# First linear of both MLPs: input parts side by side under the high weights, blocks of 256 outputs

## The chip, the cores and the metric

One NeuronCore of a Trainium2 chip runs the whole program. The metric is the device time of one execution in microseconds. Of the kernel before there are three timed runs, and one more execution was recorded by the hardware profiler.

## What is computed

Two layers of an encoder trunk on 256 tokens of width 2048 in float32. Each layer is a mixer (layer 0: a long convolution beside gated linear attention; layer 1: RWKV-7) followed by an MLP of width 8192. The change is in the MLPs:

```python
def adaln(x, c, norm_g, ada_w, ada_b):
    m = jax.nn.silu(c) @ ada_w + ada_b
    shift, scale, gate = jnp.split(m[:, None, :], 3, axis=-1)
    return rmsnorm(x, norm_g) * (1.0 + scale) + shift, gate

def sqrelu_mlp(h, w1, w2):
    return jnp.square(jax.nn.relu(h @ w1)) @ w2
...
        h, gate = adaln(x, c, ffn_norm_g[layer], ffn_ada_w[layer], ffn_ada_b[layer])
        x = x + gate * sqrelu_mlp(h, ffn_w1[layer], ffn_w2[layer])
```

Here h is 256 x 2048, w1 is 2048 x 8192 and w2 is 8192 x 2048. "First linear" is h @ w1, "second linear" is the product with w2.

## The kernel before

**Products in three parts.** The large matmuls run on operands of type float32r. So that little is lost, each float32 operand is split into a high part (a cast to float32r on ScalarE, line 465) and a low part (the float32 value minus the high part, line 466, on VectorE for weights and on GpSimd for activations). A product is then three matmuls that add up in PSUM: high x high, high x low and low x high. The function `prod` writes them (lines 504, 505, 506). Every matmul loads its own 128x128 of stationary operand first.

**Normalised input.** `norm_steps` (line 419 and on) makes h transposed, features on the partitions: 16 tiles of 128 features x 256 tokens. Eight steps make two tiles each: transposing matmuls (line 439), the high part by ScalarE (line 453), the full value by VectorE (line 457), and the low part by GpSimd (line 458). Before the change the high parts of tiles 0 to 7 lie in one buffer, their low parts in another, and tiles 8 to 15 in two more.

**First linear.** `ffn` goes through the 8192 hidden features in two halves. In each half `feat_block` makes eight blocks of 512 outputs. A block holds two PSUM buffers (tiles named f_mm), each with two groups of 128 outputs x 256 tokens; the pool has four such buffers. For each of eight loads (`load`, 512 KB: two input tiles x 512 outputs) `parts` splits the weights into f_wh and f_wl (rings of three buffers), and `feat_tiles` runs 2 input tiles x 4 output groups x 3 matmuls, each 256 columns wide: the weights are the stationary operand, and the 256 tokens move. When a block is done, each PSUM buffer (128x512) goes through ReLU on ScalarE (line 1668), a square on VectorE (line 1669), and the split into the hidden tiles f_hid (cast on ScalarE, subtract on GpSimd).

**Second linear.** After each half, `tok_block` makes four blocks of 512 outputs from that half's hidden features. There the hidden tiles are stationary and 512 weight columns move. `residual` multiplies by the gate and adds to x (lines 547, 548).

**Work beside it.** The conditioning vectors (the matrix products of `adaln` with c) are made by VectorE from streamed weights: one multiply-and-sum over 128x1024 per half row block (line 362). `tick` gives them out at a rate per load, 1.5 per two loads in layer 0's MLP and 0.8 in layer 1's, and `behind` places them after the last weight subtract. Weights and conditioning weights come over one DMA queue on SyncE.

**Order.** The code is written in one stream; a planner with a timeline of its own puts the instructions of each engine in order (`schedule_with_timeline_sim=True`, in `kernel`), held by `issue_after` marks where the code sets them. On the chip each engine runs its list in that order.

Of the kernel before, what the change touches and what calls it, by code (L numbers as in the profile page):

```python
# [10 lines left out]
F32R = mybir.dt.float32r  # L11
AF = mybir.ActivationFunctionType
ALU = mybir.AluOpType
# [3 lines left out]
P = 128  # L17
T = 256
D = 2048
KT = D // P  # L20
NB = 512
KG = 4
FF = 8192
EPS = 1e-6
# [16 lines left out]
TK, HK, HS, DV = 4, 0, 4, -12.0  # L41


def _weight_blocks(w):
    k, n = w.shape
    return w.reshape(k // (KG * P), KG, P, n // NB, NB).transpose(3, 0, 2, 1, 4)


def _cols(v):
# [75 lines left out]
def layout(i):  # L125
    a = {}
    a["x"] = np.asarray(i["x"])[0]
    rows = lambda w: np.asarray(w).T.reshape(3 * KT, P, 2, D // 2)
    a["ada_mix"] = rows(i["mix_ada_w"][0])
    a["ada_f0"] = rows(i["ffn_ada_w"][0])  # L130
    a["ada_tm"] = rows(i["tm_ada_w"][0])
    a["ada_f1"] = rows(i["ffn_ada_w"][1])
    a["c"] = np.asarray(i["c"])
    for l in range(2):
        a[f"w1_{l}"] = _weight_blocks(np.asarray(i["ffn_w1"])[l])
        a[f"w2_{l}"] = _weight_blocks(np.asarray(i["ffn_w2"])[l])
    bias = {
        "mix": np.asarray(i["mix_ada_b"])[0],
        "f0": np.asarray(i["ffn_ada_b"])[0],
        "tm": np.asarray(i["tm_ada_b"])[0],  # L140
        "f1": np.asarray(i["ffn_ada_b"])[1],
    }
    gain = {
        "mix": np.asarray(i["mix_norm_g"])[0],
        "f0": np.asarray(i["ffn_norm_g"])[0],
        "tm": np.asarray(i["tm_norm_g"])[0],
        "f1": np.asarray(i["ffn_norm_g"])[1],
    }
    win = np.asarray(i["ab_w_in"])[0]
    a["w_in"] = _weight_blocks(win[:, :6144])  # L150
    z16 = np.zeros((D, 16), np.float32)
    z80 = np.zeros((D, 80), np.float32)
    wlr = np.concatenate([win[:, 6144:6160], z16, win[:, 6160:6176], z80], axis=1)
    a["w_lr"] = wlr.reshape(KT, P, P).transpose(1, 0, 2)
    a["w_out"] = _weight_blocks(np.asarray(i["ab_w_out"])[0])
    a["hy_w3"] = np.asarray(i["hy_ffn_w3"])[0]
    a["hy_dec"] = np.asarray(i["hy_decay"])
    a["hy_skip"] = np.asarray(i["hy_skip"])[0]
    ku, kb = np.asarray(i["gla_up"])[0], np.asarray(i["gla_up_b"])[0]
    zp = np.zeros((15, 512), np.float32)  # L160
    a["gla_up"] = np.concatenate([ku[0], kb[0][None], zp, ku[1], kb[1][None]], axis=0)
    pk = _Pack()
    pk.add("ident", np.eye(P, dtype=np.float32))
    for s in SUBS:
        pk.add(f"ab_{s}", _cols(bias[s]))
        pk.add(f"g_{s}", _cols(gain[s]))
    cw = np.asarray(i["hy_conv_w"])[0]
    for j in range(3):
        pk.add(f"cw{j}", _cols(cw[j]))
    pk.add("cb", _cols(np.asarray(i["hy_conv_b"])[0]))  # L170
    pk.add("gla_g", _cols(np.asarray(i["gla_norm_g"])[0]))
    for n in ("rw_gn_g", "rw_gn_b"):
        pk.add(n, _cols(np.asarray(i[n])[0]))
    pk.add("rw_r_k", np.asarray(i["rw_r_k"])[0].reshape(KT, P).T)
    for j in range(6):
        pk.add(f"mu{j}", _cols(np.asarray(i["rw_mu"])[0, j]))
    pk.add("kk", _cols(np.asarray(i["rw_k_k"])[0]))
    pk.add("ka", _cols(np.asarray(i["rw_k_a"])[0]))
    a["pv"] = pk.array()
    rk = _Pack()  # L180
    rk1 = _Pack()
    for n, v in _rwkv_constants().items():
        (rk1 if n[:3] == "cum" else rk).add(n, v)
    a["rc"], a["rc1"] = rk.array(), rk1.array()
    for n in "rkv":
        a[f"rw_{n}"] = _weight_blocks(np.asarray(i[f"rw_w_{n}"])[0])
    a["rw_o"] = _weight_blocks(np.asarray(i["rw_w_o"])[0])
    l1, l2 = np.asarray(i["rw_w1"])[0], np.asarray(i["rw_a1"])[0]
    lo = np.concatenate([l1[0], l1[1], l2[0], l2[1], np.asarray(i["rw_g1"])[0]], axis=1)
    a["rw_lo"] = lo.reshape(8, 2, P, 640).transpose(0, 2, 1, 3)  # L190
    up = []
    for w, b in (("rw_w2", "rw_w0"), ("rw_a2", "rw_a0")):
        w, b = np.asarray(i[w])[0], np.asarray(i[b])[0]
        for d in range(2):
            up.append(np.concatenate([w[d], b[d][None]], axis=0))
    up = np.stack(up, axis=1).reshape(97, 4, 8, T).transpose(2, 0, 1, 3)
    a["rw_up"] = np.concatenate([up, np.zeros((8, 15, 4, T), np.float32)], axis=1)
    a["rw_g2"] = np.asarray(i["rw_g2"])[0].reshape(2, P, 4, NB).transpose(2, 1, 0, 3)
    hk = _Pack()
    for n in ("hy_ffn_b1", "hy_freq1", "hy_ffn_b2", "hy_freq2"):  # L200
        hk.add(n, np.asarray(i[n])[0][:, None])
    hk.add("hy_w1", np.asarray(i["hy_ffn_w1"])[0])
    hk.add("hy_w2", np.asarray(i["hy_ffn_w2"])[0])
    for n, v in _hyena_constants().items():
        hk.add(n, v)
    for n, v in _gla_constants().items():
        hk.add(n, v)
    a["hc"] = hk.array()
    a["fg"] = np.asarray(i["final_norm_g"]).reshape(1, D)
    a = {k: np.ascontiguousarray(v, dtype=v.dtype) for k, v in a.items()}  # L210
    return a, {**pk.at, "hc": hk.at, "rc": rk.at, "rc1": rk1.at}


class Build:
# [198 lines left out]
    def norm_t(self, s, split=True):  # L413
        h, step = self.norm_steps(s, split)
        for k2 in range(KT // 2):
            step(k2)
        return (lambda k: [a[:, k % 8, :] for a in h[k // 8]]) if split else h

    def norm_steps(self, s, split=True):
        nc = self.nc  # L420
# [5 lines left out]
        if s != "mix":  # L426
            self.hold = [d.ins, HK, HS]
        if split:
            h = [[self.t(self.hp, [P, KT // 2, T], "h", dt=F32R) for _ in range(2)] for _ in range(2)]
        else:  # L430
            h = [self.t(self.hp, [P, KT // 2, T], "h") for _ in range(2)]

        def step(k2):
            sh, gs = self.need(s, 0, 2 * k2 + 1), self.need(s, 1, 2 * k2 + 1)
            pt = self.t(self.ps, [P, 2, T], "ps")
            for q in range(2):
                k = 2 * k2 + q
                for j in range(2):
                    nc.tensor.matmul(pt[:, q, j * P : (j + 1) * P], lhsT=self.x[:, j, k * P : (k + 1) * P], rhs=dg[:, j, :], start=True, stop=True)  # L439
            if not split:  # L440
                for q in range(2):
                    k = 2 * k2 + q
# [4 lines left out]
                        nc.vector.tensor_scalar(o, pt[:, q, :], gs[:, k : k + 1], sh[:, k : k + 1], ALU.mult, ALU.add)  # L447
                return
            u = self.t(self.tmp, [P, 2, T], "u")
            hi, lo = (a[:, 2 * k2 % 8 : 2 * k2 % 8 + 2, :] for a in h[k2 // 4])  # L450
            for q in range(2):
                k = 2 * k2 + q
                nc.scalar.activation(hi[:, q, :], pt[:, q, :], AF.Identity, bias=sh[:, k : k + 1], scale=gs[:, k : k + 1])
# [32 lines left out]

    def load(self, name, n, i, pools):

        self.turn += 1
        w = self.t(pools[self.turn % len(pools)], [P, 2, NB], "w")  # L490
        self.dma = self.nc.sync.dma_start(w, self.A[name][n, i // 2][:, i % 2 * 2 : i % 2 * 2 + 2]).ins
        self.tick(self.rate / 2)
        return w

# [21 lines left out]
    def feat_block(self, name, n, act, pools):  # L516
        pt = [self.t(self.mm, [P, 2, T], "mm") for _ in range(2)]
        for i in range(KT // 2):
            self.feat_tiles(pt, i, self.parts(self.load(name, n, i, pools)), act)
        return pt  # L520

    def tok_block(self, name, n, ks, act, pools):
# [336 lines left out]
    def mix(self):  # L859
        nc = self.nc  # L860
        yq = self.ctx.enter_context(ExitStack())
        yp = self.pool(yq, "yp", bufs=4, reuse_waits="tile")
        with ExitStack() as st:
            self.lp = self.pool(st, "lp")
            bp = self.pool(st, "bp", bufs=13, reuse_waits="tile")
            n = self.A["hc"].shape[1]
# [7 lines left out]
            self.bg(n=FX)  # L874
            self.load_x()
            h, norm = self.norm_steps("mix")
            lhs = lambda k: [a[:, k % 8, :] for a in h[k // 8]]
            self.starting, self.spc = True, TF
            first = {n: [self.t(self.mm, [P, 2, T], "mm") for _ in range(2)] for n in (0, 2)}
            if NF == 3:  # L880
# [770 lines left out]
    def ffn(self, s):  # L1651
        nc = self.nc
        l = int(s[1])
        with ExitStack() as st:
            hid_p = self.pool(st, "hid", bufs=8, reuse_waits="tile")
            wx = self.pool(st, "wx", bufs=7, reuse_waits="tile")
            pools = [(self.wp, wx)[int(i)] for i in PT[l]]
            self.due = DU if l else DV
            h = self.norm_t(s)
            for half in range(2):  # L1660
                hid = []
                for n in range(8):
                    if n % 2 == 0:
                        hid.append([self.t(hid_p, [P, 8, T], "hid", dt=F32R) for _ in range(2)])
                    pt = self.feat_block(f"w1_{l}", 8 * half + n, h, pools)
                    for q in range(2):
                        u = self.t(self.tmp, [P, 2, T], "u")
                        nc.scalar.activation(u, pt[q], AF.Relu)
                        nc.vector.tensor_tensor(u, u, u, ALU.mult)
                        c = slice((n % 2) * 4 + 2 * q, (n % 2) * 4 + 2 * q + 2)  # L1670
                        self.split(u, *(a[:, c, :] for a in hid[-1]), nc.gpsimd)
                act = lambda k: [a[:, k % 8, :] for a in hid[k // 8 - 4 * half]]
                for n in range(D // NB):
                    pt = self.tok_block(f"w2_{l}", n, (32 * half, 32 * half + 32), act, pools)
                    self.residual(s, n, pt, half == 1)
# [43 lines left out]
```

## Time and profile before

| | us |
|---|---|
| median of three runs | 3032.49 |
| lowest and highest run | 3032.04, 3037.37 |
| the profiled execution | 3034.37 |
| its span, first to last instruction | 3032.4 |
| layer 0's MLP in it | about 655 to 1360 |
| layer 1's MLP in it | about 2289 to 3032 |

In the rows, PE is TensorE's matmuls and PEld its weight loads, DVE is VectorE, ACT is ScalarE, POOL is GpSimd. A name such as f_mm is that of a tile with its number left out; f_ stands for the MLP of either layer, mix_ and tm_ for the mixers of layers 0 and 1. A group's row gives line, engine, operation, what is written from what, shape and count, then the busy time in us and the mean duration of one in ns, then the idle time of the engine just ahead of such instructions and what ended it. Matmuls overlap one another, and their ends are modelled: their spacing is read from their starts. A row of the waits gives the total in us, how many times, and the longest. In the windows the count of instructions stands behind each engine's busy time.

### The profile page before, as it was taken

The page shows a single profiled execution, that of the slowest core. Times are in us where ns is not written, and L with a number is a line of the kernel's source. Part 1 is how long each engine was busy: PE and PEld are TensorE (multiplying, and loading weights), DVE is VectorE, ACT ScalarE, POOL GpSimd, SP SyncE. Part 2 cuts the span into 40 slices and gives each one's busy share as a digit, 9 for nine tenths or more (in the row PEclk, how much of TensorE's full clock was granted, in tenths as well). Part 3 has the DMA queues.
Part 4 walks back from the last instruction along what each step waited for, and adds up shares of the span by engine and source line. Part 5 has one row for each costly group of instructions (what it writes and reads, how often), then busy time and mean ns, then how long its engine had stood idle before and what let it go on. Part 6 is the DMA issues. An engine that isn't in the chain of part 4 may idle for free. (4 is left out here: it accounts for less than half of the span.)

```text
span 3032.4 us, 52074 instructions
## 1 busy us (share of the span) xinstructions
PE 2861.2 (94%) x20308; PEld 2481.7 (82%) x20308; DVE 2114.9 (70%) x3126; ACT 1301.1 (43%) x1947; POOL 514.6 (17%) x574
## 2 busy tenths in 40 slices
PE   5998989999999999997998988999998999999998
PEld 2678776789988999886888876887778998899986
DVE  7888877657887888887758875555556676455454
ACT  3233344444443444443466552444445443344443
POOL 1211200011100011004344441222322110001000
PEclk9999999999999999999999996999999999999999
DMA  9977687747999999994988887865545777555552
GB/s 314 334 274 273 230 276 257 260 156 269 313 321 335 336 326 319 334 332 144 327 255 261 265 270 213 247 201 164 146 154 197 246 254 271 194 184 185 201 193 92
DMA packets 279970, 752.30 MB, mean 248 GB/s; under 512 B 73081, under 2 KB 99577, under 8 KB 278572
## 3 DMA queue, kind: packets, MB, share of 16 engines
q1 hardware_dynamic: 279148, 745.38, 73.3%
q8 instruction: 159, 2.61, 0.4%
q10 hardware_dynamic: 576, 3.60, 0.3%
q14 instruction: 87, 0.71, 0.1%
HBM read 706.08 MB, written 42.80 MB: 247 GB/s over the span
## 5 line engine op out<-in xcount | busy, mean ns | idle before, releaser
L466 DVE TENSOR_TENSOR f_wl<-f_w,f_wh 128x1024 fp32r<-128x1024 f32 x512 | 633.7, 1239 | 412.7 <-ACT f_wh L465 408.3
L465 ACT CAST f_wh<-f_w 128x1024 fp32r<-128x1024 f32 x512 | 537.7, 1052 | 744.0 <-PE f_mm L506 316.4
L505 PE MATMUL f_mm<-f_h,f_wh 128*128 128x256 f32 x2048 | 579.7, 283 | 0.0
L504 PE MATMUL f_mm<-f_h,f_wh 128*128 128x256 f32 x2048 | 579.5, 283 | 0.0
L506 PE MATMUL f_mm<-f_h,f_wl 128*128 128x256 f32 x2048 | 578.9, 283 | 0.0
L505 PE MATMUL f_mm<-f_wl,f_hid 128*128 128x512 f32 x1024 | 398.7, 389 | 0.6 <-DVE f_wl L466 0.6
L506 PE MATMUL f_mm<-f_wh,f_hid 128*128 128x512 f32 x1024 | 398.4, 389 | 0.0
L505 PEld LDWEIGHTS f_mm<-f_h,f_wh 128*128 128x128 f32 x2048 | 393.2, 192 | 0.1
L504 PEld LDWEIGHTS f_mm<-f_h,f_wh 128*128 128x128 f32 x2048 | 393.0, 192 | 0.1
L506 PEld LDWEIGHTS f_mm<-f_h,f_wl 128*128 128x128 f32 x2048 | 392.9, 192 | 0.0
L504 PE MATMUL f_mm<-f_wh,f_hid 128*128 128x512 f32 x1024 | 357.8, 389 | 0.0
L362 DVE SCALAR_TENSOR_TENSOR f_w<-f_w,mix_s 128x1024 f32<-128x1024 f32 x209 | 275.1, 1317 | 1.7 <-DMA f_w<-in_ada_f 1.7
L362 DVE SCALAR_TENSOR_TENSOR mix_w<-mix_w,mix_s 128x1024 f32<-128x1024 f32 x175 | 220.5, 1269 | 76.6 <-DMA mix_w<-in_ada_f 49.2
L466 POOL TENSOR_TENSOR f_hid<-f_u,f_hid 128x512 fp32r<-128x512 f32 x64 | 94.2, 1472 | 995.4 <-ACT f_hid L465 990.5
L505 PEld LDWEIGHTS f_mm<-f_wl,f_hid 128*128 128x128 f32 x1024 | 192.2, 188 | 41.1 <-DVE f_wl L466 1.4
L506 PEld LDWEIGHTS f_mm<-f_wh,f_hid 128*128 128x128 f32 x1024 | 192.2, 188 | 39.9
L504 PEld LDWEIGHTS f_mm<-f_wh,f_hid 128*128 128x128 f32 x1024 | 192.2, 188 | 39.8
L466 DVE TENSOR_TENSOR tm_wl<-tm_w,tm_wh 128x1024 fp32r<-128x1024 f32 x128 | 164.9, 1290 | 85.3 <-ACT tm_wh L465 82.1
L465 ACT CAST mix_wh<-mix_w 128x1024 fp32r<-128x1024 f32 x114 | 119.4, 1050 | 206.8 <-PE mix_mm L506 90.3
L504 PE MATMUL tm_mm<-tm_x,tm_wh 128*128 128x256 f32 x512 | 160.6, 314 | 11.8 <-DMA tm_x<-mix 11.3
L466 DVE TENSOR_TENSOR mix_wl<-mix_w,mix_wh 128x1024 fp32r<-128x1024 f32 x114 | 142.4, 1254 | 38.8 <-ACT mix_wh L465 38.6
L465 ACT CAST tm_wh<-tm_w 128x1024 fp32r<-128x1024 f32 x128 | 133.4, 1045 | 83.5 <-PE tm_mm L505 61.3
(452 smaller groups left out, 5415.8 us busy)
## 6 DMA issues: line engine op xcount, KB each, us to landing
f_w<-in_w SPq DMA_DIRECT2D x512, 512.0 KB, 5.1
f_w<-in_ada_f SPq DMA_DIRECT2D x128, 512.0 KB, 5.8
mix_w<-in_ada_mix SPq DMA_DIRECT2D x96, 512.0 KB, 6.3
f_w<-in_ada_tm SPq DMA_DIRECT2D x81, 512.0 KB, 6.0
mix_w<-in_w_in SPq DMA_DIRECT2D x80, 512.0 KB, 5.1
mix_w<-in_ada_f SPq DMA_DIRECT2D x64, 512.0 KB, 5.3
tm_x<-mix SPq DMA_DIRECT2D x64, 512.0 KB, 5.7
mix_w<-in_w_out SPq DMA_DIRECT2D x32, 512.0 KB, 4.7
```

What stands on the lines that cost most here:

```text
L362: V.scalar_tensor_tensor(w, w, 1.0, self.s[:, j * (D // 2) : (j + 1) * (D // 2)], ALU.mult, ALU.mult, accum_out=a[:, j, i : i + 1])
L465: self.nc.scalar.copy(hi, a)
L466: d = (eng or self.nc.vector).tensor_tensor(lo, a, hi, ALU.subtract)
L504: mm(out, lhsT=l[0], rhs=r[0], start=start, stop=False)
L505: mm(out, lhsT=l[0], rhs=r[1], start=False, stop=False)
L506: mm(out, lhsT=l[1], rhs=r[0], start=False, stop=stop)
```

## The change

The weights of the first linear are laid out in blocks of 256 outputs, so that a load (still 512 KB) brings four input tiles x 256 outputs. The normalised input lies in four buffers of four tiles each, the high and the low part of a tile side by side, 512 columns. `feat_pair` takes the place of `feat_block` in `ffn`: for each input tile and 128 outputs, one matmul of the high weights with all 512 columns, whose result fills a PSUM buffer (first half: high x high, second half: high x low), and one matmul of the low weights with the 256 columns of the high part, added to the first half. When the pair of 128 outputs is done, ScalarE copies the second half of each buffer, VectorE adds the first half to the copy, and one VectorE instruction makes max(u, 0) x u, which is the squared ReLU. The mixer of layer 0 reads the same new layout of its normalised input, with its matmuls unchanged.

```diff
-NB = 512
+NB, NH = 512, 256
...
-def _weight_blocks(w):
+def _weight_blocks(w, nb=NB):
     k, n = w.shape
-    return w.reshape(k // (KG * P), KG, P, n // NB, NB).transpose(3, 0, 2, 1, 4)
+    return w.reshape(k // (KG * P), KG, P, n // nb, nb).transpose(3, 0, 2, 1, 4)
...
-        a[f"w1_{l}"] = _weight_blocks(np.asarray(i["ffn_w1"])[l])
+        a[f"w1_{l}"] = _weight_blocks(np.asarray(i["ffn_w1"])[l], NH)
...
-        return (lambda k: [a[:, k % 8, :] for a in h[k // 8]]) if split else h
+        return (lambda k: h[k // 4][:, k % 4]) if split else h
...
-            h = [[self.t(self.hp, [P, KT // 2, T], "h", dt=F32R) for _ in range(2)] for _ in range(2)]
+            h = [self.t(self.hp, [P, KT // 4, 2, T], "h", dt=F32R) for _ in range(4)]
...
-            hi, lo = (a[:, 2 * k2 % 8 : 2 * k2 % 8 + 2, :] for a in h[k2 // 4])
+            hi, lo = (h[k2 // 2][:, 2 * k2 % 4 : 2 * k2 % 4 + 2, a] for a in range(2))
...
+        return self.fetch(self.A[name][n, i // 2][:, i % 2 * 2 : i % 2 * 2 + 2], [P, 2, NB], pools)
+
+    def fetch(self, src, shape, pools):
         self.turn += 1
-        w = self.t(pools[self.turn % len(pools)], [P, 2, NB], "w")
-        self.dma = self.nc.sync.dma_start(w, self.A[name][n, i // 2][:, i % 2 * 2 : i % 2 * 2 + 2]).ins
+        w = self.t(pools[self.turn % len(pools)], shape, "w")
+        self.dma = self.nc.sync.dma_start(w, src).ins
         self.tick(self.rate / 2)
         return w
...
+    def feat_pair(self, name, n, act, pools):
+
+        mm = self.nc.tensor.matmul
+        pt = [self.t(self.mm, [P, 2, T], "mm") for _ in range(2)]
+        for i in range(KT // 4):
+            hi, lo = self.parts(self.fetch(self.A[name][n, i], [P, 4, NH], pools))
+            for j in range(4):
+                k = 4 * i + j
+                x = act(k)
+                for q in range(2):
+                    c = slice(q * P, (q + 1) * P)
+                    mm(pt[q], lhsT=hi[:, j, c], rhs=x, start=k == 0, stop=False)
+                    mm(pt[q][:, 0], lhsT=lo[:, j, c], rhs=x[:, 0], start=False, stop=k == KT - 1)
         return pt
...
-                for n in range(8):
-                    if n % 2 == 0:
+                for n in range(16):
+                    if n % 4 == 0:
                         hid.append([self.t(hid_p, [P, 8, T], "hid", dt=F32R) for _ in range(2)])
-                    pt = self.feat_block(f"w1_{l}", 8 * half + n, h, pools)
+                    pt = self.feat_pair(f"w1_{l}", 16 * half + n, h, pools)
+                    u = self.t(self.tmp, [P, 2, T], "u")
                     for q in range(2):
-                        u = self.t(self.tmp, [P, 2, T], "u")
-                        nc.scalar.activation(u, pt[q], AF.Relu)
-                        nc.vector.tensor_tensor(u, u, u, ALU.mult)
-                        c = slice((n % 2) * 4 + 2 * q, (n % 2) * 4 + 2 * q + 2)
-                        self.split(u, *(a[:, c, :] for a in hid[-1]), nc.gpsimd)
+                        nc.scalar.copy(u[:, q], pt[q][:, 1])
+                        nc.vector.tensor_tensor(u[:, q], pt[q][:, 0], u[:, q], ALU.add)
+                    nc.vector.scalar_tensor_tensor(u, u, 0.0, u, ALU.max, ALU.mult)
+                    c = slice((n % 4) * 2, (n % 4) * 2 + 2)
+                    self.split(u, *(a[:, c, :] for a in hid[-1]), nc.gpsimd)
```

More of the change, by code (lines that the diff above doesn't have):

```diff
@@ L519, in feat_block @@
             self.feat_tiles(pt, i, self.parts(self.load(name, n, i, pools)), act)
+        return pt
+    def feat_pair(self, name, n, act, pools):
[10 more added lines that the diff above has]
+                    mm(pt[q][:, 0], lhsT=lo[:, j, c], rhs=x[:, 0], start=False, stop=k == KT - 1)
         return pt
@@ L876, in mix @@
             h, norm = self.norm_steps("mix")
-            lhs = lambda k: [a[:, k % 8, :] for a in h[k // 8]]
+            lhs = lambda k: [h[k // 4][:, k % 4, a] for a in range(2)]
             self.starting, self.spc = True, TF
```

## The prediction

> **What bounds the kernel now.** I read the page's first two parts for the busy engines and the clock, then the windows view inside the four stretches of the first linear, then the timeline of TensorE for the spacing of its matmuls, and last the waits of TensorE and VectorE.
>
> ```profile
> span 3032.4 us, 52074 instructions
> PE 2861.2 (94%) x20308; PEld 2481.7 (82%) x20308; DVE 2114.9 (70%) x3126; ACT 1301.1 (43%) x1947; POOL 514.6 (17%) x574
> ...
> L505 PE MATMUL f_mm<-f_h,f_wh 128*128 128x256 f32 x2048 | 579.7, 283 | 0.0
> L504 PE MATMUL f_mm<-f_h,f_wh 128*128 128x256 f32 x2048 | 579.5, 283 | 0.0
> L506 PE MATMUL f_mm<-f_h,f_wl 128*128 128x256 f32 x2048 | 578.9, 283 | 0.0
> ```
>
> The first linear is 3 x 2048 = 6144 matmuls of 256 columns, the three groups at the bottom; their 283 ns overlap, so they are no price. The windows (busy time of PE, PEld, DVE, ACT, POOL, then clock, DMA share, GB/s) show the first linear of layer 0 (two stretches), that of layer 1, and for contrast a second linear of layer 0:
>
> ```profile
> 700.00:840.00 140.00, 140.00 (x1171) 140.00 (x1170) 117.46 (x149) 64.18 (x75) 17.47 (x12) 1.00 0.89 303
> 1070.00:1210.00 140.00, 140.00 (x1162) 139.70 (x1161) 118.18 (x146) 64.99 (x76) 17.42 (x12) 1.00 0.93 321
> 2310.00:2460.00 150.00, 150.00 (x1253) 150.00 (x1252) 98.51 (x100) 67.99 (x78) 17.82 (x12) 1.00 0.70 233
> ...
> 880.00:1020.00 140.00, 140.00 (x619) 115.74 (x618) 115.03 (x154) 54.45 (x52) 0.00 (x0) 1.00 0.93 337
> ```
>
> TensorE is busy in all of each window at the full granted clock (1.00). VectorE is next: 84% in layer 0 (117.46 of 140), 66% in layer 1. TensorE's waits, from layer 0's MLP to its end, then from layer 1's MLP to its end, say the same:
>
> ```profile
> PE f_ps L439 <- issue: 4.4, 1, 4.4
> ...
> PE f_ps L439 <- DVE f_dg L425: 7.9, 1, 7.9
> PE f_mm L505 <- DVE f_wl L466: 0.6, 1, 0.6
> ```
>
> Only the starts of the stages and one 0.6 us wait stand in these answers, none inside a first linear. What shortens TensorE's stream there shortens the kernel, until something else is late.
>
> **The price of one matmul.** Two timeline stretches of TensorE, the first in a first linear, the second in a second linear. Between the two quoted starts lie 36 matmul steps in each (a line with x2 counts twice).
>
> ```profile
> 1037.73 0.28 PE L505 MATMUL f_mm<-f_h,f_wh 128*128 128x256 f32 x1
> ...
> 1042.05 0.28 PE L505 MATMUL f_mm<-f_h,f_wh 128*128 128x256 f32 x1
> ```
> ```profile
> 1217.80 0.39 PE L506 MATMUL f_mm<-f_wh,f_hid 128*128 128x512 f32 x1
> ...
> 1225.95 0.39 PE L506 MATMUL f_mm<-f_wh,f_hid 128*128 128x512 f32 x1
> ```
>
> 4.32 us / 36 = 120.0 ns for 256 columns, 8.15 us / 36 = 226.4 ns for 512. The line through both is 0.4156 ns a column and 13.6 ns fixed per matmul with its weight load. So two narrow matmuls cost 240.0 and one wide one 226.4.
>
> **The change on TensorE.** For each of 16 input tiles and 128 outputs the kernel has three matmuls of 256: 360.0 ns. After it, one of 512 (high weights against both input parts) and one of 256 (low weights against the high part): 226.4 + 120.0 = 346.4 ns. Both still load new weights each time. There are 2048 such groups (2 layers x 64 output tiles x 16), so 2048 x 13.6 ns = 27.8 us go, 13.9 in each layer. A pair of output tiles falls from 11.52 to 11.08 us, and the 64 pairs from 737 to 709 us.
>
> The trace has no 256 matmul that follows a 512 one with the loads alternating so. Bounds for it: a weight load today fits behind a 256 matmul at 120.0 ns, so it does not cost more; at best it costs half of the wide one, 113.2, if 13.6 ns of the 120 is the load and now hides behind the wide matmul before it. That would take 2048 x 6.8 = 13.9 us more. I take 120.0, since the load of the high weights has only the narrow matmul to hide behind, as today.
>
> The Trainium skill speaks against the size of this: TensorE: Matmul & The Clock Gate, section "Back-to-back issue gap", gives N/2.4 + 2.5 ns for a warm isolated matmul, a fixed part of only 2.5 ns, by which the change would save an estimated 2048 x 2.5 ns = 5 us. The trace disagrees: 120.0 and 226.4 leave 13.6.
>
> **Eviction.** Before, a 128x512 result takes one Relu on ScalarE, a square on VectorE, a cast on ScalarE and a subtract on GpSimd. After it, ScalarE copies the two second halves, VectorE adds them to the first halves (two 128x256 with one PSUM operand), then one VectorE instruction does max and multiply; cast and subtract stay. 64 results either way. Prices from the groups:
>
> ```profile
> L1668 ACT ACTIVATE f_u<-f_mm 128x512 f32<-128x512 f32 x64 | 38.0, 594 | 42.2 <-PE f_mm L506 42.2
> L1612 ACT COPY tm_o<-tm_ps 128x256 f32<-128x256 f32 x16 | 6.0, 372 | 8.9 <-PE tm_ps L1609 8.8
> L1669 DVE TENSOR_TENSOR f_u<-f_u 128x512 f32<-128x512 f32 x64 | 59.3, 926 | 11.0 <-ACT f_u L1668 11.0
> L1159 DVE SCALAR_TENSOR_TENSOR tm_h<-tm_h,tm_h 128x512 f32<-128x512 f32 x8 | 7.7, 966 | 0.0
> L668 DVE SCALAR_TENSOR_TENSOR mix_b<-mix_mm,mix_pv,mix_b 128x255 f32<-128x255 f32 x24 | 11.1, 475 | 4.1 <-ACT mix_b L667 4.1
> L1645 DVE TENSOR_TENSOR tm_o<-tm_o,tm_ps 128x256 f32<-128x256 f32 x16 | 6.7, 419 | 11.8 <-PE tm_ps L1643 8.4 <-POOL tm_o L1640 3.2
> ```
>
> ScalarE: 2 x 372 - 594 = +0.15 us a pair, nothing to an engine that is 46% busy. The max-and-multiply stands for the square at the same price (966 against 926). VectorE: two adds of 419 to 475 ns, +0.84 to +0.95, say +0.89 us a pair. Layer 1: 98.51/150 x 11.52 = 7.57 us a pair becomes 8.46 of 11.08; covered. Layer 0: 117.46/140 x 11.52 = 9.67 becomes 10.56 of 11.08, 95%. That is tight. The cover there is what VectorE idles now:
>
> ```profile
> DVE f_wl L466 <- ACT f_wh L465: 24.2, 31, 2.3
> DVE f_u L1669 <- ACT f_u L1668: 0.7, 2, 0.4
> ```
>
> (window 700 to 850): 24.2 us in which it is ahead and waits for a buffer of split weights to come free, 1.86 a pair, harmless. What is new is that VectorE stands in order at the first add until ScalarE has copied, and ScalarE until TensorE has finished. Behind the add stand the weight subtracts (1.24 us each) and the conditioning products (1.32). ScalarE's wait of this kind is today 42.2/64 = 0.66 us a result. Three buffers of split weights give 2 x 2.77 us of lead, of which cast and subtract take 1.05 + 1.24, so 3.25 us are left:
>
> ```profile
> L466 DVE TENSOR_TENSOR f_wl<-f_w,f_wh 128x1024 fp32r<-128x1024 f32 x512 | 633.7, 1239 | 412.7 <-ACT f_wh L465 408.3
> L465 ACT CAST f_wh<-f_w 128x1024 fp32r<-128x1024 f32 x512 | 537.7, 1052 | 744.0 <-PE f_mm L506 316.4
> L362 DVE SCALAR_TENSOR_TENSOR f_w<-f_w,mix_s 128x1024 f32<-128x1024 f32 x209 | 275.1, 1317 | 1.7 <-DMA f_w<-in_ada_f 1.7
> ```
>
> An eviction (0.89 + 0.93) with one product (1.32) is 3.14 us, just inside, and 0.66 of waiting puts it just outside. At the lower bound this costs nothing; with 0.66 us added to each pair layer 0 would need 11.22 instead of 11.08, 32 x 0.14 = 4.5 us. I take 3.
>
> **Starts of the two stages.** The block is now 256 outputs wide, so the first pair wants all 16 input tiles in 11.1 us, not in 23, and the wide matmul wants the low part at once. GpSimd makes the low parts:
>
> ```profile
> L458 POOL TENSOR_TENSOR f_h<-f_u,f_h 128x512 fp32r<-128x512 f32 x16 | 22.1, 1409 | 194.9 <-DVE f_u L457 194.9
> ```
>
> Eight in a row take 11.3 us against TensorE's 11.1, and they start ahead of it: nothing, up to 2 us a stage if one is late. I take 1 for both stages.
>
> **Loads.** Same count and size (512 KB, 256 loads for the two layers), same queue. A load now has 2.77 us, not 2.88, so 303 to 321 GB/s become 315 to 334, still under the 337 at which the second linear runs without a wait. Zero. PSUM: a pair holds two of four buffers and must be evicted within the next pair's 11.1 us; about 3 us are needed. Zero. The other stages only see another layout of the normalised input, with the same instructions.
>
> **Sum.** -27.8 + 3 + 1 = -23.8 us. The profiled execution took 3034.37 (span 3032.4 and 2.0 around it), 1.9 above the median of the runs, 3032.49. So 3010.6 for such an execution, and 3008.7 from the median: **3008.7**.
>
> **Rivals.**
>
> VectorE takes over layer 0. For it: 95% without waits. Against: 1.86 us of idle a pair to spend. If VectorE needed as much as TensorE's old 11.52, layer 0 would gain nothing and layer 1 its 13.9, less 1 for the starts: 3019.6. Chance 0.12.
>
> Slower: the in-order adds hold VectorE back. If at each pair of layer 0 VectorE reached its add early and stood for 2.3 us, the longest wait it shows now, it would need 10.56 + 2.3 = 12.86 us a pair, 1.34 over the old 11.52: +42.9 in layer 0, -13.9 in layer 1, about +30 with the starts, 3062. It decides from the point where the wait eats layer 1's gain too: (11.52 + 0.43 - 10.56) = 1.39 us a pair. Against: the square waits only 0.7 us in 13 results now. Chance 0.05.
>
> The weight load hides better: the narrow matmul at 113.2 gives 13.9 us more, 2994.8. For it: the longer cover before. Against: the other load has no longer one. Chance 0.08.
>
> No fixed part to save: if the 13.6 ns came from alternating operands or banks and stayed per 256 columns, the wide matmul here would take 240 and only the eviction's cost would stay, 3036 at most, 3032 without it. The second linear's 226.4 speaks against it, on the same tiles and loads. Chance 0.04. By the page of the Trainium skill named above, TensorE: Matmul & The Clock Gate, an estimated 5 us would still be saved, 3031.
>
> **How the numbers follow.** Forecast 0.71; its own range is 3004 (no late VectorE) to 3014. A measurement of this kernel tells about 0.2%, 6 us, from no change. Faster: 0.71 + 0.12 + 0.08 = 0.91, same 0.04, slower 0.05. The range takes in VectorE's takeover, to 3020, and half of the bound on the narrow matmul, to 3000; what is left out is about 0.2.
>
> **What would show it.** In the changed profile: two groups of 2048 f_mm matmuls on f_h, one of 512 and one of 256 columns, with starts 226 and 120 ns apart in turn; some 808 matmuls in a window of 140 us, where 1171 and 1162 stand now; adds of 0.42 to 0.48 us; VectorE near 95% in layer 0's first linear and 76% in layer 1's; waits of TensorE for f_wl of at most some us. Wrong: a step of 240 ns for the wide matmul, or tens of us of TensorE waiting for f_wl or for f_mm buffers.

## The result, and the profile after

The changed kernel takes 3011.02 us (median of four runs, 3007.85 to 3016.40), the kernel before beside it 3032.26: 21.2 us less, ratio 0.9927, 95% interval 0.9909 to 0.9945. The forecast was 3008.7. The profiled execution took 3007.85 with a span of 3005.8. From its page, the busy engines and the two groups of the first linears (for groups: count, then busy us and mean ns):

```profile
PE 2830.1 (94%) x18260; PEld 2361.8 (79%) x18260; DVE 2153.2 (72%) x3254; ACT 1302.3 (43%) x2011; POOL 535.7 (18%) x574
...
L536 PE MATMUL f_mm<-f_h,f_wh 128*128 128x512 f32 x2048 | 709.1, 396 | 0.0
L537 PE MATMUL f_mm<-f_h,f_wl 128*128 128x256 f32 x2048 | 554.2, 279 | 0.0
```

Three groups of 2048 narrow matmuls became one of wide and one of narrow ones. The windows inside the first linears (layer 0 twice, then layer 1), columns as before:

```profile
700.00:840.00 140.00, 140.00 (x811) 122.43 (x810) 128.67 (x179) 66.20 (x89) 21.84 (x12) 1.00 0.90 313
1050.00:1190.00 140.00, 140.00 (x806) 122.19 (x805) 129.61 (x170) 66.72 (x89) 21.24 (x13) 1.00 0.91 323
2310.00:2450.00 140.00, 140.00 (x807) 122.20 (x806) 103.54 (x130) 65.91 (x87) 22.83 (x13) 1.00 0.75 245
```

TensorE still has no gap in these windows. VectorE is at 92 and 93% in layer 0 (128.67 and 129.61 of 140) and at 74% in layer 1. The counts of 806 to 811 hold against the predicted 808.

The cleanest measure of the change is the length of one half of a first linear, from its first matmul to the first one of the second linear that follows. For layer 0's second half, the timeline of TensorE, before and then after:

```profile
1023.93 0.28 PE L504 MATMUL f_mm<-f_h,f_wh 128*128 128x256 f32 x1
...
1208.25 0.40 PE L504 MATMUL f_mm<-f_wh,f_hid 128*128 128x512 f32 x1
```
```profile
1019.18 0.39 PE L536 MATMUL f_mm<-f_h,f_wh 128*128 128x512 f32 x1
...
1197.48 0.40 PE L507 MATMUL f_mm<-f_wh,f_hid 128*128 128x512 f32 x1
```

184.32 us became 178.30. The second half of a layer starts straight after a second linear, with all input tiles long made; these halves are called clean below, since the start of the stage is not in them. All four halves, read in the same way:

| us | layer 0, first | layer 0, second | layer 1, first | layer 1, second | sum |
|---|---|---|---|---|---|
| before | 191.52 | 184.32 | 190.19 | 184.31 | 750.34 |
| after | 185.61 | 178.30 | 182.29 | 179.18 | 725.38 |

Between the two profiled executions the time fell by 26.5 us; 25.0 of that lie in the first linears. The second linears kept their length (174.23 and 174.13 us for layer 0's first). The last matmul of layer 0's MLP starts at 1382 us in the trace before, so the 1360 in the table ahead of the prediction is too early; no length here uses it.

### The profile page after: what moved, and what is told of

Read it like the earlier page. It is cut to its first block, busy times and chain, and to the rows that moved or that the text cites. A ratio compares the mean times of both kernels' runs of the same rounds, so it can differ in the third digit from the quotient of the medians.

```text
span 3005.8 us, 48118 instructions
## 1 busy us (share of the span) xinstructions
PE 2830.1 (94%) x18260; PEld 2361.8 (79%) x18260; DVE 2153.2 (72%) x3254; ACT 1302.3 (43%) x2011; POOL 535.7 (18%) x574
## 4 chain that ended last, share of the span: by engine, by line
PE 73%; DMA 10%; DVE 10%; issue 3%; ACT 2%; POOL 1%; SPq 1%; DVEq 0%; ACTq 0%; POOLq 0%
PE f_mm L536 16%; PE f_mm L537 8%; PE f_mm L508 8%; PE f_mm L507 8%; PE f_mm L509 8%; DMA mix_w<-in_ada_f 4%; PE tm_mm L507 3%; PE tm_mm L508 2%; PE tm_mm L509 2%; DMA mix_w<-in_ada_mix 2%; DVE mix_w L362 2%; PE mix_mm L508 2%; PE mix_mm L509 2%; PE mix_mm L507 2%; DVE mix_wl L466 1%
## 5 line engine op out<-in xcount | busy, mean ns | idle before, releaser
L536 PE MATMUL f_mm<-f_h,f_wh 128*128 128x512 f32 x2048 | 709.1, 396 | 0.0
L537 PE MATMUL f_mm<-f_h,f_wl 128*128 128x256 f32 x2048 | 554.2, 279 | 0.0
L536 PEld LDWEIGHTS f_mm<-f_h,f_wh 128*128 128x128 f32 x2048 | 377.1, 188 | 81.9
L537 PEld LDWEIGHTS f_mm<-f_h,f_wl 128*128 128x128 f32 x2048 | 385.5, 188 | 9.1
L362 DVE SCALAR_TENSOR_TENSOR f_w<-f_w,mix_s 128x1024 f32<-128x1024 f32 x209 | 291.3, 1395 | 1.9 <-DMA f_w<-in_ada_f 1.9
L466 POOL TENSOR_TENSOR f_hid<-f_u,f_hid 128x512 fp32r<-128x512 f32 x64 | 115.7, 1808 | 956.7 <-ACT f_hid L465 890.8
L507 PE MATMUL tm_mm<-tm_x,tm_wh 128*128 128x256 f32 x512 | 158.3, 310 | 2.8 <-DMA tm_x<-mix 2.8
L509 PE MATMUL tm_mm<-tm_x,tm_wl 128*128 128x256 f32 x512 | 149.0, 294 | 2.7 <-DVE tm_wl L466 2.7
L508 PE MATMUL tm_mm<-tm_x,tm_wh 128*128 128x256 f32 x512 | 150.2, 294 | 0.0
```

The source lines that it names most:

```text
L362: V.scalar_tensor_tensor(w, w, 1.0, self.s[:, j * (D // 2) : (j + 1) * (D // 2)], ALU.mult, ALU.mult, accum_out=a[:, j, i : i + 1])
L466: d = (eng or self.nc.vector).tensor_tensor(lo, a, hi, ALU.subtract)
L507: mm(out, lhsT=l[0], rhs=r[0], start=start, stop=False)
L508: mm(out, lhsT=l[0], rhs=r[1], start=False, stop=False)
L509: mm(out, lhsT=l[1], rhs=r[0], start=False, stop=stop)
L536: mm(pt[q], lhsT=hi[:, j, c], rhs=x, start=k == 0, stop=False)
```

## The experiments

The theory was: each matmul has a fixed part of 13.6 ns beside its columns, one matmul of three is saved, and nothing else is late. Rivals were that the eviction on VectorE takes part of it back, and that a wide and a narrow matmul in turn cost something of their own, since 178.30 us over 512 groups are 348.2 ns a group (one wide and one narrow matmul) and 179.18 are 350.0, not 346.4. All kernels below are edits of the changed kernel unless said otherwise, and each was timed beside the kernel before.

**All of the change but the wide matmul.**

```diff
-                    mm(pt[q], lhsT=hi[:, j, c], rhs=x, start=k == 0, stop=False)
+                    mm(pt[q][:, 0], lhsT=hi[:, j, c], rhs=x[:, 0], start=k == 0, stop=False)
+                    mm(pt[q][:, 1], lhsT=hi[:, j, c], rhs=x[:, 1], start=False, stop=False)
```

> The changed kernel with its layout, its blocks of 256 and its copy and add at the end, but three matmuls of 256 columns as before: the wide one is split into its halves. Theory (only the width of the matmul brings the time, the rest of the change costs nothing): 360.0 ns a group, 184.3 us a half as before, time within 3 us of 3032. Rival (copy, add and the narrower blocks cost some us and the wide matmul brings more than it seems): 3036 or more.

3037.99 us, ratio 1.0015 (1.0005 to 1.0024). Layer 0's second half:

```profile
1022.06 0.28 PE L536 MATMUL f_mm<-f_h,f_wh 128*128 128x256 f32 x1
...
1206.37 0.40 PE L507 MATMUL f_mm<-f_wh,f_hid 128*128 128x512 f32 x1
```

184.31 us, the length of before to 0.01, and 749.89 in the four halves. So with narrow matmuls the new blocks, layout and eviction leave the first linears as they were; the gain there comes with the width. The 4 us more lie outside the first linears, which I had not expected.

**Without the adds, and with a ReLU of the same size in place of each copy.**

```diff
-                        nc.scalar.copy(u[:, q], pt[q][:, 1])
-                        nc.vector.tensor_tensor(u[:, q], pt[q][:, 0], u[:, q], ALU.add)
-                    nc.vector.scalar_tensor_tensor(u, u, 0.0, u, ALU.max, ALU.mult)
+                        nc.scalar.activation(u[:, q], pt[q][:, 0], AF.Relu)
+                    nc.vector.tensor_tensor(u, u, u, ALU.mult)
```

> The changed kernel without the copies and adds: ScalarE applies ReLU to the first halves alone, VectorE squares; the product of high weights and low input is still made and then left out of the result. VectorE has 0.84 us a pair less to do. Theory (VectorE at 93% in layer 0 never holds TensorE): the time of the changed kernel, 3011, within 3 us, halves of the first linear at 178 to 179 us. Rival (the adds hold TensorE back by some us in layer 0): 3 to 5 us less, all of it in layer 0.

3015.45 us, ratio 0.9942 (0.9921 to 0.9962). VectorE has less to do in layer 0 (113.39 of 140 us, was 129.61), and TensorE's stream does not notice:

```profile
1050.00:1190.00 140.00, 140.00 (x805) 122.14 (x804) 113.39 (x147) 67.55 (x88) 20.68 (x13) 1.00 0.94 332
```
```profile
1025.15 0.39 PE L536 MATMUL f_mm<-f_h,f_wh 128*128 128x512 f32 x1
...
1203.45 0.40 PE L507 MATMUL f_mm<-f_wh,f_hid 128*128 128x512 f32 x1
```

178.30 us again, and 179.18 in layer 1. The adds cost nothing in the time. ScalarE's two instructions a pair are still there (67.55 us busy, was 66.72), so this kernel does not price the copies; no row shows TensorE waiting for them.

**Two more instructions on VectorE at each eviction.**

```diff
+                    for _ in range(2):
+                        nc.vector.scalar_tensor_tensor(u, u, 0.0, u, ALU.max, ALU.max)
                     nc.vector.scalar_tensor_tensor(u, u, 0.0, u, ALU.max, ALU.mult)
```

> The changed kernel with two more instructions on VectorE at each eviction, max(max(u, 0), u) over 128x512, which leave the later result as it is, some 0.69 us each: 1.37 us a pair. VectorE is busy 10.3 of the 11.14 us of a pair in layer 0 and 8.6 to 9 in layer 1. Theory (VectorE has 0.8 us a pair left in layer 0 and then takes over): it would need 11.7 us, TensorE waits 0.56 us at each of 32 pairs, the halves of layer 0 grow to some 187 us, 18 us in all, and layer 1 stays at 179. Rival (the ring of split weights takes up the lag and VectorE's load does not matter): 178 to 179 us in both layers, time 3011.

3023.71 us, ratio 0.9976 (0.9959 to 0.9993), 10 us over the changed kernel run beside it. Layer 0 twice, then layer 1, and TensorE's waits in layer 0:

```profile
700.00:840.00 140.00, 139.23 (x797) 119.83 (x796) 137.71 (x194) 63.50 (x87) 19.95 (x11) 1.00 0.89 303
1050.00:1190.00 140.00, 138.85 (x787) 119.21 (x786) 139.00 (x191) 63.35 (x85) 22.18 (x12) 1.00 0.91 315
2320.00:2460.00 140.00, 140.00 (x806) 122.16 (x805) 112.12 (x149) 66.95 (x89) 20.19 (x12) 1.00 0.75 240
```
```profile
PE f_mm L536 <- ACT f_wh L465: 2.1, 1, 2.1
PE f_mm L537 <- DVE f_wl L466: 1.3, 3, 0.7
PE f_mm L508 <- DVE f_wl L466: 1.0, 2, 0.5
```

VectorE is full in layer 0 (139.00 of 140), TensorE runs 787 matmuls where it ran 806, and waits for split weights stand in the list of layer 0, where the changed kernel has none. Layer 1 keeps its 806 in the window, but its second half took 180.1 us, 0.9 more. The rival "VectorE takes over layer 0" is a real one, and the changed kernel stands less than these 1.4 us a pair away from it. The price was about 11 us, not 18: layer 0's halves came to 187.1 and some 186 us, as expected, but only the second had stood at 178.3 before; the first had stood at 185.6. Another 2 us lie in the second linear between them. The listed waits make up 4.4 us of the price.

**Order of the wide and narrow matmuls.** In groups of two (both wide ones of an input tile, then both narrow ones) and in groups of eight (all wide ones of a load first):

```diff
                 for q in range(2):
                     c = slice(q * P, (q + 1) * P)
                     mm(pt[q], lhsT=hi[:, j, c], rhs=x, start=k == 0, stop=False)
+                for q in range(2):
+                    c = slice(q * P, (q + 1) * P)
                     mm(pt[q][:, 0], lhsT=lo[:, j, c], rhs=x[:, 0], start=False, stop=k == KT - 1)
```

> For each input tile the two wide matmuls come first, then the two narrow ones. In the changed kernel a wide and a narrow matmul in turn take 348 to 350 ns, where the rows of before give 226.4 + 120.0 = 346.4. Theory A (a matmul costs its columns and a fixed part, whatever stands beside it, and the rest is scatter): the halves of the first linear stay at 178 to 179 us, the time at 3011. Theory B (each change of width costs): half of the changes go, so half of the 2 to 4 ns, 0.5 to 0.9 us a half, 2 to 4 us in all. Theory C (the narrow matmul pays for adding to the bank that the wide one has just written): all of it goes, 177.4 us a half, 4 to 6 us in all.

> Per load, all eight wide matmuls come first, then all eight narrow ones: one change of width each way per load in place of eight. Theory A: 178 to 179 us a half, 3011. Theory B: nearly all of the excess goes, 177.5 us a half, 4 to 6 us in all, more than with groups of two. Theory C: the same as with groups of two. TensorE also needs the low weights 1.8 us later, which would only help if it waited for them, and it does not.

3015.41 us, ratio 0.9949 (0.9932 to 0.9966), and 3014.86, ratio 0.9938 (0.9921 to 0.9955). The clean halves of layers 0 and 1 are 178.33 and 178.33 us in groups of two, 178.73 and 178.75 in groups of eight: 348.3 and 349.1 ns a group. Neither B nor C: with an eighth of the changes of width the excess over 346.4 is still there. In groups of eight it is not at the changes at all: the steps there take 226.8 and 120.0 ns in layer 0's clean half, while those from a wide matmul to the next wide one take 230.5 in the mean.

**One PSUM buffer at a time, and all matmuls wide.**

```diff
-            for j in range(4):
-                k = 4 * i + j
-                x = act(k)
-                for q in range(2):
-                    c = slice(q * P, (q + 1) * P)
+            for q in range(2):
+                c = slice(q * P, (q + 1) * P)
+                for j in range(4):
+                    k = 4 * i + j
+                    x = act(k)
```

> The two output groups are the outer loop within a load: four input tiles in turn go to one PSUM buffer, then four to the other, where the changed kernel goes to the other buffer after every two matmuls. From the runs so far a wide matmul among wide ones takes 229 to 230 ns in the first linear, in the second linear 226.4; there six matmuls in turn go to one buffer. Theory D (going to the other PSUM buffer costs the wide matmul its 3 ns): 346.4 ns a group, 177.4 us a half, 4 to 6 us less in all four halves together. Rival E (it is where the operands lie, or what is read with them, not the buffer): 178 to 179 us a half as in the changed kernel.

3013.12 us, ratio 0.9939 (0.9921 to 0.9957); clean halves of 179.09 and 180.86 us, longer than the changed kernel's 178.30 and 179.18. Going to the other buffer is not what costs. In the other kernel the low weights too take all 512 columns, which adds the product of the two low parts:

```diff
-                    mm(pt[q][:, 0], lhsT=lo[:, j, c], rhs=x[:, 0], start=False, stop=k == KT - 1)
+                    mm(pt[q], lhsT=lo[:, j, c], rhs=x, start=False, stop=k == KT - 1)
```

> The low weights too are multiplied with all 512 columns, which adds the product low x low to the second half (the reference's value a little more exactly). All matmuls of the first linear are wide, two a group. If a wide matmul costs here what it costs in the second linear: 2 x 226.4 = 452.8 ns, 231.8 us a half, some 213 us more than the changed kernel in all. If it costs 229 to 230 wherever it stands in the first linear: 458 to 460 ns, 234.5 to 235.5 us a half, 224 to 228 us more. If it is the mixing of widths that costs 2 to 4 ns: the first of the two.

3231.91 us, ratio 1.066 (1.0637 to 1.0684). Layer 0's second half:

```profile
1072.16 0.39 PE L536 MATMUL f_mm<-f_h,f_wh 128*128 128x512 f32 x1
...
1304.27 0.39 PE L507 MATMUL f_mm<-f_wh,f_hid 128*128 128x512 f32 x1
```

232.11 us for 1024 matmuls, 226.7 ns each, what a wide matmul costs in the second linear. So the operands and their place alone are not to blame either: a stream of wide ones costs 226.7 each, a stream of narrow ones 120.0, and a stream of both 348 to 353 a group in the mean in place of 346.7, in every order tried.

The means hide two paces. Read load by load (eight groups), the changed kernel's clean half of layer 1 goes like this; the first two starts are one load apart, and so are the last two:

```profile
2662.35 0.40 PE L536 MATMUL f_mm<-f_h,f_wh 128*128 128x512 f32 x1
2665.12 0.40 PE L536 MATMUL f_mm<-f_h,f_wh 128*128 128x512 f32 x1
...
2670.71 0.40 PE L536 MATMUL f_mm<-f_h,f_wh 128*128 128x512 f32 x1
2673.54 0.40 PE L536 MATMUL f_mm<-f_h,f_wh 128*128 128x512 f32 x1
```

2.77 us is 8 x 346.7 ns, the plain sum of the two widths; 2.83 is 354 a group. In the clean halves 45 of 64 loads in layer 0 and 31 of 64 in layer 1 take 2.773 to 2.777 us, and nearly all the others 2.81 to 2.83. The counts are the same in a second execution, and from the seventh load on every change of pace falls at a load in which the planner has put two wide matmuls in a row. So wide and narrow in turn can add up exactly. What keeps the slower pace going was not tested.

**What lies outside the first linears.** The kernel with narrow matmuls had shown 4 us there. Three kernels: the changed one again; the changed one with the old layout in layer 0's mixer; and the kernel before with nothing but the new layout.

```diff
+            if s == "mix":
+                h = [[self.t(self.hp, [P, KT // 2, T], "h", dt=F32R) for _ in range(2)] for _ in range(2)]
+            else:
+                h = [self.t(self.hp, [P, KT // 4, 2, T], "h", dt=F32R) for _ in range(4)]
...
```

> The changed kernel once more, as the base for the others of this call. If the halves of the first linear come out at 178.3 and 179.2 us once more (second half of layer 0 and of layer 1), they are a property of the program; the rest of the time, the two mixers, may differ by some us from execution to execution. Time 3011 within 4.

> The changed kernel with the old layout of the normalised input in layer 0's mixer, the new one only in the MLPs. The kernel with all of the change but the wide matmul took 4 us more than before with its first linears unchanged, so something outside of them costs. If it is the layout in the mixer of layer 0 (its matmuls then read other addresses): 3007, 4 us under the changed kernel. If it is not: the same as the changed kernel, within 2 us.

```diff
-            h = [[self.t(self.hp, [P, KT // 2, T], "h", dt=F32R) for _ in range(2)] for _ in range(2)]
+            h = [self.t(self.hp, [P, KT // 4, 2, T], "h", dt=F32R) for _ in range(4)]
...
```

> The kernel before with the new layout of the normalised input alone: blocks of 512, three matmuls of 256, old eviction. Layout theory: 4 us over the kernel before, all outside of the first linears. Rival (the blocks of 256 or the eviction cost it, or chance): the time of the kernel before within 2 us.

Again: 3013.59 us, ratio 0.9943 (0.9925 to 0.9961), clean halves 178.30 and 179.18 to the hundredth. Old layout in the mixer: 3011.73, 0.9944 (0.9928 to 0.9960). Layout alone: 3032.81, 1.0007 (0.9997 to 1.0016). The layout costs nothing that can be told. Most of the scatter sits in layer 1's mixer: from the start of layer 0's last second linear to the first matmul of layer 1's MLP the eight profiled executions that share the changed kernel's order there (the changed kernel twice, the old layout in the mixer, and the edits without adds, with more on VectorE, and in three other orders) took 1083.1 to 1100.3 us, the three with the old order (before, layout alone, narrow) 1085.9 to 1090.9. (The stages ahead of layer 0's MLP took 656.6 to 665.9 in the eight.) One stretch of 115 us in that part, the changed kernel, then the one without adds:

```profile
1831.00:1946.00 115.00, 109.50 (x1318) 92.26 (x1319) 71.53 (x174) 43.64 (x104) 22.20 (x40) 0.95 0.86 248
```
```profile
1838.00:1953.00 115.00, 109.69 (x1150) 92.92 (x1148) 63.55 (x155) 37.24 (x87) 20.96 (x40) 0.82 0.74 227
```

The same order of instructions at a granted clock of 0.95 and 0.82: 1318 matmuls against 1150, so the count falls to 0.87 and the clock to 0.86. The second execution was the longer one by 17 us in this part, of 23 in all. What lowers the clock was not tested.

## Why the prediction was right

**TensorE.** The step said 2048 x 13.6 ns = 27.8 us. The clean halves gave 6.0 and 5.1 us where 7.0 each were due, so 22.3 us in all four halves, taking a first half's stream to gain what the second one does; the rest of the 25.0 is the starts, below. The mechanism is shown: with narrow matmuls nothing is gained (184.31), and one wide matmul in place of two narrow ones is what saves. That the saving is a fixed part of each matmul is a reading: two widths always lie on a line. Its size is 13.3 ns, since whole halves give 226.7 for a wide matmul (232.11 us / 1024) where 36 steps had given 226.4; that makes 27.3 us. The 5 us between that and 22.3 are the loads at the slower pace: 348.2 and 350.0 ns a group in the mean for 346.7. The case of a better hidden weight load can be struck: in the clean halves the step from a narrow start to the next wide one is 116 ns in the mean, but the step from wide to narrow grew to 233 to 234, and no pace goes below the sum of the two.

The estimate of 5 us by the Trainium skill's page TensorE: Matmul & The Clock Gate, section "Back-to-back issue gap", falls: the first linears alone lost 25.0.

**Eviction.** I put 3 us of lateness in layer 0; it was nothing, as the kernel without the adds shows: its halves there are 185.1 and 178.3 us, against 185.6 and 178.3. The prices held (adds 418 ns, copies 374), except that max-and-multiply took 686 ns where I had 926 to 966, so VectorE came to 93% and not 95%:

```profile
L1687 DVE TENSOR_TENSOR f_u<-f_mm,f_u 128x256 f32<-128x256 f32 x128 | 53.5, 418 | 20.3 <-ACT f_u L1686 20.0
L1688 DVE SCALAR_TENSOR_TENSOR f_u<-f_u 128x512 f32<-128x512 f32 x64 | 43.9, 686 | 1.0
L1686 ACT COPY f_u<-f_mm 128x256 f32<-128x256 f32 x128 | 47.8, 374 | 89.6 <-PE f_mm L537 89.6
```

The feared wait, VectorE at the add until ScalarE has copied, was 20.0 us over 128 adds, 0.16 each.

**Starts.** I put +1; a first half takes longer than a second one by 7.2 and 5.9 us before, by 7.3 and 3.1 after. So -2.7, in layer 1; why it got shorter there was not tested.

**Sum.** The three terms came to -22.3 + 0 - 2.7 = -25.0 in the first linears, where I had -23.8. That the two sums are so close is luck: the stream gave 5.5 us less than the step said, and the eviction and the starts cost 6.7 less than I put. The gain and its cause were right, the three sizes were not. For the profiled pair the total was -26.5. The medians differ by 21.2, some 4 us less than the first linears gave; that much lies outside them, where two executions of one program differ by more (1083.1 and 1091.8 us for the changed kernel in the part above). Whether the planner's other order of layer 1's mixer costs some us of its own, and where the narrow kernel's 4 us lie, these runs do not settle.

The early rivals: VectorE taking over did not happen, and needs 1.4 us a pair or less to begin; the slower case and the case without a fixed part are excluded by the halves; the better hidden load as well.

## What to carry to other kernels

Read the spacing of starts for two widths of the same matmul: what two narrow ones take beyond one wide one, times the number of merges, is the gain while TensorE has no gap. Expect a little less of it where the widths then alternate. Then divide the next engine's work by TensorE's new time, stage by stage, since the engine at 84% before is at 93% after and the next improvement may end there. And judge a change of under 1% by the lengths of the stages it touches: the clean halves repeated here to 0.01 us, the first halves to 0.6, while the medians of one kernel differed by 2.6.

## What the runs showed of the hardware

Wide float32r matmuls with a weight load each follow at 226.7 ns, narrow ones at 120.0 (columns 512 and 256). A wide and a narrow one in turn go at two paces, 346.7 ns a group, the plain sum, or up to 354, and change from one to the other in the middle of a stage in which TensorE shows no gap; the means over a clean half lie 1.5 to 6.5 ns above the sum in the orders tried, and the cause stays open. And the granted clock of one stretch in layer 1's mixer was 0.95 in one execution and 0.82 in another with the same order of instructions; 17 of the 23 us between these two lie in the part that holds it.
